# Shorter TensorE times in the clock estimate that orders a two-layer decoder's issue

## The chip, the core and the metric

The kernel runs on one core of a Trainium2 chip. The metric is the device time of one execution in microseconds (us), the median of several runs. One further execution was recorded by the hardware profiler; all rows below come from that one. The engines are TensorE (PE; its weight loads are PEld), VectorE (DVE), ScalarE (ACT), GpSimd (POOL) and SyncE (SP), which issues the DMAs.

## What is computed

Two residual layers over x of 2048 positions and 1024 channels, `x = x + rms_norm(mixer(rms_norm(x)))` each. Layer 0 projects to 2304 columns and has two head groups: sliding-window attention (8 query heads, 2 key/value heads, window 128, ALiBi, sinks) and a pooling mixer with windows 2, 4, 8 and 16; each is gated by a SiLU, and an output projection joins them. Layer 1 is a convolution module: a projection to 3072 columns, GLU, a causal depthwise convolution of 31 taps, a LayerNorm over channels, SiLU, a SiLU gate and an output projection:

```
proj = h @ w_in
a, b, gate = split(proj)
conv = depthwise_causal_conv(a * sigmoid(b), dw_w, 31 taps) + dw_b
y = silu(layer_norm(conv)) * silu(gate)
return y @ w_out
```

All data is float32.

## The kernel before, in words

Channels lie on partitions, 128 a tile (8 tiles), and positions in the free dimension, in two halves of 1024 with two blocks of 512 each. A projection of one output tile and one block (`project`, L385) runs over the 8 input tiles and issues three matmuls for each: weights and activations are split into a high and a low float32r part, and high by high, high by low and low by high are added into one PSUM bank. So a projection has 24 matmuls of 512 columns; the last block of the kernel is done in two parts of 256 columns (`last_block`, L1011). After each group of three matmuls `flow.pump()` lets other work in.

The order of the big work is written out: layer 0 for each half (36 projections with attention and pooling, then 16 of the output), layer 1's input for each half (32 projections of 8 channel tiles for GLU, then 16 gates), then layer 1's output for each half. Everything else is a task, a Python generator with a priority: weight loads and splits (`w_load`, `w_split`, priority 0), what reads a bank (0), attention (`scores`, `weighted`, 2), post-norm (`post_norm`, 1), the norm of the convolution (`norms`, L1158, 1 and 2), the convolution. Five of the eight channel tiles are convolved on DVE (`conv_dve`, L1027, priority 4: 31 taps over 128x1024, the first two as tensor_scalar, then 29 multiply-adds, and a sum), three on TensorE with Toeplitz matrices loaded by DMA (`conv_pe`, L1048, priority 2). `norms` of a half needs that half's convolution for all 8 tiles, sums them, takes the mean with matmuls and gives the input of the output projection, which waits for it tile by tile through `ready`.

The instructions are issued in the order in which this program calls them, each engine's in a queue of its own, with no other reordering. That order is decided by `Flow`, a running estimate of each engine's clock. Every operation's call adds its cost (`Engine.cost`, L156) to its engine's clock, not before its inputs' estimated ends (`note`, L78); it returns the estimated end, and a task yields that time. `once` (L123) goes through the tasks by priority and runs the first that is allowed:

```
ready = task[3]
if ready is not None and ready + MARGIN > self.t["P"]:
    continue
if task[0] > 0 and max(self.t["V"], self.t["A"]) > self.t["P"] + LAG:
    continue
```

Here `t["P"]`, `t["V"]` and `t["A"]` are the clocks of TensorE, DVE and ACT, MARGIN is 0.2 us and LAG 1.0 us. `wait` (L141), with which the main order waits for buffers and inputs, runs tasks until its condition holds and moves TensorE's clock on when none may run. The costs are in us. Beside TensorE's: a DVE operation on n elements a partition costs 0.063 + 1.04e-3 n, plus 0.067 for each per-partition scalar operand, half the slope for copies and tensor_scalar in SBUF; a DMA is taken as landed 0.65 + bytes/360e3 + 0.95 us after its issue if the queue is free (384 KB: 1.09 us in the middle).

All engine calls go through one helper, so every instruction of the profile has the line L189; tiles are told apart by name: `mm` a projection's bank, `wh` and `wl` split weights, `s` general tiles, `a`, `pt`, `pv` banks of attention, statistics and convolution, `in_toep` the Toeplitz matrices.

Of the kernel before, what the change touches and what calls it, by code (L numbers as in the profile page):

```python
# [53 lines left out]
class Flow:  # L54
# [17 lines left out]
    def keys(ap):  # L72
# [3 lines left out]
        return [(ap.name, c) for c in range(lo // 256, hi // 256 + 1)]  # L76

    def note(self, e, cost, ins, outs):  # L78
        s = self.t[e]
        for x in ins:  # L80
# [71 lines left out]
class Engine:  # L152
# [3 lines left out]
    def cost(self, op, out, ins, kw):  # L156
        n = 1
        for d in out.shape[1:]:
            n *= d
        psum = any(x.space == PSUM for x in ins + [out])  # L160
        ptr = 0.067 * sum(1 for x in ins if n > 1 and x.shape[-1] == 1)
        if self.key == "P":
            if op == "transpose":
                return 0.109
            f = ins[0].dtype
            if f == F32R:
                return max(0.111, 0.007 + 0.224 * n / 512)
            if n * out.shape[0] < 256:
                return 0.108
            part = 0.56 if out.shape[0] == 64 else 1.0  # L170
            return part * n * 1.74e-3
        if self.key == "V":
            if op == "reciprocal":
                return 0.06 + n * 6.25e-3
            fast = op in ("tensor_copy", "tensor_scalar") and not psum
            return 0.063 + ptr + n * (0.52e-3 if fast else 1.04e-3)
        if self.key == "A":
            return (0.052 if psum else 0.093) + 1.4 * ptr + n * 0.833e-3 + (0.09 if kw.get("accum_out") is not None else 0.0)
        if kw.get("op") == ALU.pow:
            return 1.0  # L180
        if op == "tensor_tensor":
            return 0.1 + n * 2.2e-3
        return 0.1 + n * 3.4e-3
# [1162 lines left out]
```

## Time and profile before

| | us |
|---|---|
| median of 3 runs (1518.21 to 1519.53) | 1518.54 |
| the profiled execution, its own time | 1523.78 |
| its span, first to last instruction | 1521.2 |
| TensorE busy in the span | 1477.2 |
| DVE busy | 1247.4 |
| ACT busy | 564.4 |
| GpSimd busy | 56.8 |

The span is what the trace shows; the profiled execution's own time has a little around it, and the unprofiled runs are somewhat shorter. Matmuls are pipelined, so the mean duration of one record is longer than the step from one to the next; the step is read from long pieces of the chain of waits. "x" is a count. A float32 matmul (not float32r) leaves two records. The release of a wait (`<-`) names what came last.

### The profile page before, as it was taken

What the parts mean: (1) busy time and instruction counts of PE and PEld (TensorE: products, weight loads), DVE (VectorE), ACT (ScalarE), POOL (GpSimd) and SP (SyncE); (2) the same over time, 40 slices, a digit from 0 to 9 for tenths busy, and PEclk for the clock granted to TensorE, in tenths of its full rate; (3) what the DMA queues carried; (4) which work ended last, traced back from release to release, by engine and by line L of the source; (5) the groups of instructions that cost most, each with busy time, mean ns of one, the idle gap of its engine ahead of it and who ended that gap; (6) DMA issues with size and microseconds to landing.
All of it is one profiled execution on the core that took longest, in us unless ns stands there. A gap on an engine that the chain in (4) does not pass through costs nothing.

```text
span 1521.2 us, 19133 instructions
## 1 busy us (share of the span) xinstructions
PE 1477.2 (97%) x7226; PEld 1192.8 (78%) x7226; DVE 1247.4 (82%) x1927; ACT 564.4 (37%) x1069; POOL 56.8 (4%) x65
## 2 busy tenths in 40 slices
PE   8999999999999999999999999999899999999997
PEld 6777788787777778787788878888788788788887
DVE  7887775776877755576799999969999799899975
ACT  6455422554444323454211113311112235375541
POOL 0000000000000000000100000000000002000000
PEclk9999999999999999999999999999999999999998
DMA  6122112464411111355421234431644654846764
GB/s 223 47 91 96 44 44 60 137 189 157 142 32 32 41 33 56 104 174 180 155 61 62 69 88 161 125 97 42 192 133 133 190 184 134 250 156 191 238 221 140
DMA packets 107468, 186.46 MB, mean 123 GB/s; under 512 B 32240, under 2 KB 56432, under 8 KB 107376
## 3 DMA queue, kind: packets, MB, share of 16 engines
q1 hardware_dynamic: 107376, 185.25, 38.7%
q8 instruction: 56, 0.92, 0.3%
q14 instruction: 36, 0.29, 0.1%
HBM read 146.42 MB, written 38.80 MB: 122 GB/s over the span
## 4 chain that ended last, share of the span: by engine, by line
PE 65%; DVE 23%; DMA 6%; issue 3%; ACT 2%; SPq 1%; POOL 0%; POOLq 0%; DVEq 0%; ACTq 0%
PE mm L189 56%; DVE s L189 18%; PE a L189 4%; PE pv L189 3%; DVE wl L189 2%; PE pt L189 2%; DVE t L189 2%; DMA s<-in_toep 2%; DMA xr<-in_xp 1%; ACT s L189 1%; SPq L189 1%; ACT t L189 1%; DMA gt<-s 1%; DMA xr<-x 1%; ACT wh L189 0%
## 5 line engine op out<-in xcount | busy, mean ns | idle before, releaser
L189 PE MATMUL mm<-s,wh 128*128 128x512 f32 (+1 forms) x3616 | 1138.6, 396 | 9.7 <-ACT s L189 6.2
L189 PEld LDWEIGHTS mm<-s,wh 128*128 128x128 f32 x3616 | 669.7, 189 | 159.3 <-ACT s L189 7.8
L189 PE MATMUL mm<-s,wl 128*128 128x512 f32 (+1 forms) x1808 | 710.9, 393 | 0.5 <-DVE wl L189 0.5
L189 PEld LDWEIGHTS mm<-s,wl 128*128 128x128 f32 x1808 | 341.6, 189 | 77.5 <-DVE wl L189 0.9
L189 DVE SCALAR_TENSOR_TENSOR s<-s,packed,s 128x1024 f32<-128x1024 f32 x290 | 354.3, 1282 | 0.0
L189 ACT ACTIVATE wh<-wr 128x1024 fp32r<-128x1024 f32 (+1 forms) x138 | 145.2, 1052 | 349.0 <-PE mm L189 319.7
L189 DVE TENSOR_TENSOR wl<-wr,wh 128x1024 fp32r<-128x1024 f32 (+1 forms) x138 | 167.5, 1214 | 82.3 <-ACT wh L189 82.1
L189 ACT ACTIVATE t<-mm 128x512 f32<-128x512 f32 (+1 forms) x122 | 68.6, 562 | 107.2 <-PE mm L189 94.0
L189 PE MATMUL a<-s,s 128*128 128x128 f32 (+2 forms) x592 | 94.9, 297 | 10.9 <-DMA s<-in_toep 8.1
L189 DVE TENSOR_TENSOR t<-t,t 128x512 f32<-128x512 f32 (+1 forms) x131 | 85.8, 662 | 20.0 <-ACT t L189 18.2
L189 PEld LDWEIGHTS a<-s,s 128*128 128x128 f32 x592 | 82.6, 194 | 24.8 <-DMA s<-in_toep 11.7
L189 DVE TENSOR_TENSOR s<-s,s 128x512 f32<-128x512 f32 (+3 forms) x100 | 85.3, 873 | 6.9 <-DMA s<-sg 2.1
L189 ACT ACTIVATE s<-t 128x512 fp32r<-128x512 f32 (+1 forms) x52 | 48.8, 938 | 110.1 <-DVE t L189 109.6
L189 ACT ACTIVATE s<-mm 128x512 f32<-128x512 f32 (+1 forms) x116 | 67.9, 586 | 52.1 <-PE mm L189 49.0
L189 ACT ACTIVATE t<-s 128x512 f32<-128x512 f32 x80 | 49.3, 629 | 58.7 <-DVE s L189 50.3
L189 DVE TENSOR_TENSOR s<-t,s 128x512 fp32r<-128x512 f32 (+1 forms) x56 | 52.1, 930 | 23.1 <-ACT s L189 22.1
L189 DVE TENSOR_TENSOR t<-pt,packed 128x512 f32<-128x512 f32 x64 | 44.2, 690 | 31.4 <-PE pt L189 31.2
L189 POOL TENSOR_TENSOR rs<-ms,mhalf 128x4 f32<-128x4 f32 (+1 forms) x21 | 29.4, 1398 | 800.4 <-DVE ms L189 800.4
L189 ACT ACTIVATE s<-s,st 128x128 f32<-128x128 f32 x128 | 49.7, 390 | 22.2 <-DVE st L189 22.0
L189 DVE SCALAR_TENSOR_TENSOR s<-t,mm 128x512 f32<-128x512 f32 x48 | 39.9, 831 | 14.9 <-PE mm L189 13.7
L189 ACT ACTIVATE s<-xh 128x512 fp32r<-128x512 f32 x48 | 30.2, 632 | 51.2 <-DVE xh L189 50.6
L189 DVE TENSOR_TENSOR s<-s,xr 128x512 f32<-128x512 f32 x56 | 37.5, 687 | 7.5 <-DMA xr<-x 4.7
(100 smaller groups left out, 917.9 us busy)
## 6 DMA issues: line engine op xcount, KB each, us to landing
wr<-in_wo SPq DMA_DIRECT2D x64, 512.0 KB, 3.7
wr<-in_wc SPq DMA_DIRECT2D x48, 512.0 KB, 3.7
wr<-in_wa SPq DMA_DIRECT2D x27, 512.0 KB, 3.8
s<-in_toep SPq DMA_DIRECT2D x24, 384.0 KB, 4.5
xr<-in_xp SPq DMA_DIRECT2D x32, 256.0 KB, 4.0
x<-s SPq DMA_DIRECT2D x32, 256.0 KB, 3.1
xh<-x SPq DMA_DIRECT2D x32, 256.0 KB, 3.1
sg<-s SPq DMA_DIRECT2D x16, 512.0 KB, 5.0
```

The source lines that it names most:

```text
L189: fn(*args, **kw)
```

## The change

In the cost of a TensorE operation the three constants of the matmuls are replaced; the cost of a transpose (0.109) and of the smallest matmuls (0.108) stay, and so do all costs of the other engines, MARGIN, LAG and all instructions.

```diff
             f = ins[0].dtype
             if f == F32R:
-                return max(0.111, 0.007 + 0.224 * n / 512)
+                return max(0.107, 0.2148 * n / 512)
             if n * out.shape[0] < 256:
                 return 0.108
             part = 0.56 if out.shape[0] == 64 else 1.0
-            return part * n * 1.74e-3
+            return part * n * 1.67e-3
```

## Rows read from the trace of the kernel before

**Rows 1.** The page's first part: busy us, share of the span, instructions.

```profile
PE 1477.2 (97%) x7226; PEld 1192.8 (78%) x7226; DVE 1247.4 (82%) x1927; ACT 564.4 (37%) x1069; POOL 56.8 (4%) x65
```

**Rows 2.** Stretches: window and length; PE, PEld, DVE, ACT, POOL busy; PEclk, DMA share, GB/s.

```profile
0.00:170.80 170.80, 161.12 (x882) 123.32 (x883) 142.93 (x403) 91.77 (x239) 5.63 (x16) 1.00 0.31 102
366.90:528.80 161.90, 159.29 (x912) 123.95 (x911) 125.25 (x361) 68.59 (x194) 2.21 (x3) 1.00 0.20 63
744.00:994.70 250.70, 246.68 (x1067) 199.06 (x1066) 250.46 (x243) 52.16 (x74) 18.92 (x15) 1.00 0.32 99
994.70:1213.60 218.90, 210.85 (x1034) 174.58 (x1032) 188.05 (x164) 38.58 (x74) 1.44 (x7) 0.99 0.43 128
1213.60:1309.90 96.30, 96.30 (x434) 77.92 (x434) 93.65 (x116) 40.75 (x68) 7.74 (x2) 1.00 0.52 168
```

**Rows 3.** The chain of waits, three undisturbed pieces: start us, us, engine and tile.

```profile
546.16 78.11 PE mm L189 x336
...
1215.22 1.34 PE a L189 x12
...
1490.22 18.43 PE mm L189 x156
```

**Rows 4.** The waits of TensorE: who, for whom, us in total, times, longest.

```profile
PE a L189 <- DMA s<-in_toep: 8.1, 8, 2.7
...
PE a L189 <- DVE s L189: 5.8, 9, 2.8
PE pv L189 <- DVE s L189: 4.4, 2, 2.5
PE mm L189 <- DVE s L189: 3.6, 4, 1.9
PE pt L189 <- DVE t L189: 3.4, 4, 1.4
```

**Rows 5.** The timeline of TensorE at two waits: start, us, instruction [idle before, releaser].

```profile
907.63 1.10 PE L189 MATMUL pv<-s,onesr 128*128 128x512 f32 x2 [2.48 <-DVE s L189]
...
1459.06 0.39 PE L189 MATMUL mm<-s,wh 128*128 128x256 f32 x1 [1.87 <-DVE s L189]
```

**Rows 6.** Groups of DVE, 768.2 to 879.3 us: count, busy us, mean ns, idle before.

```profile
L189 DVE SCALAR_TENSOR_TENSOR s<-s,packed,s 128x1024 f32<-128x1024 f32 x73 | 88.9, 1284 | 0.0
L189 DVE TENSOR_TENSOR wl<-wr,wh 128x1024 fp32r<-128x1024 f32 x10 | 12.2, 1222 | 0.0
L189 DVE SCALAR_TENSOR_TENSOR s<-t,mm 128x512 f32<-128x512 f32 x10 | 8.6, 865 | 0.0
L189 DVE TENSOR_TENSOR s<-s,s 128x1024 f32<-128x1024 f32 x2 | 4.0, 2024 | 0.1
L189 DVE TENSOR_SCALAR s<-s,packed 128x1024 f32<-128x1024 f32 x4 | 2.9, 775 | 0.0
```

**Rows 7.** The timeline of DVE before 907 us: start us, us, instruction, count.

```profile
900.41 1.04 DVE L189 SCALAR_TENSOR_TENSOR s<-t,mm 128x512 f32<-128x512 f32 x1
901.28 4.86 DVE L189 SCALAR_TENSOR_TENSOR s<-s,packed,s 128x1024 f32<-128x1024 f32 x4
906.05 1.00 DVE L189 SCALAR_TENSOR_TENSOR s<-t,mm 128x512 f32<-128x512 f32 x1
```

**Rows 8.** Three more stretches, columns as in rows 2.

```profile
1003.00:1014.00 11.00, 11.00 (x49) 8.94 (x48) 2.26 (x2) 1.55 (x2) 0.00 (x0) 1.00 0.46 168
1014.00:1205.00 191.00, 183.80 (x900) 152.15 (x898) 179.00 (x156) 32.74 (x64) 1.39 (x6) 0.99 0.43 126
1213.60:1454.80 241.20, 238.38 (x1055) 192.66 (x1055) 225.36 (x312) 127.73 (x201) 12.09 (x6) 0.99 0.61 195
```

**Rows 9.** Groups of TensorE's 512-column matmuls, 1213.6 to 1454.8 us.

```profile
L189 PE MATMUL mm<-s,wh 128*128 128x512 f32 x640 | 202.2, 397 | 0.0
L189 PE MATMUL mm<-s,wl 128*128 128x512 f32 x320 | 126.1, 394 | 0.0
```

**Rows 10.** The page's DMA issues, Toeplitz loads: count, KB, median us to landing.

```profile
s<-in_toep SPq DMA_DIRECT2D x24, 384.0 KB, 4.5
```

## The prediction, made before the change was run

> **What bounds the kernel now.** I began with the engines' shares of the span. TensorE is busy for 97% of it and VectorE (DVE) for 82% [rows 1]: the reader should take from this that no other order of issue can win much, since the matmuls stay the same. Next came the stretches between the phases [rows 2]. In the attention of layer 0 (0 to 171 us, 367 to 529 us) TensorE is idle for 9.7 and 2.6 us, the first with the start of the kernel in it, and DVE has time to spare; from 744 to 995 us, in layer 1's first projection and gates, both are nearly full, DVE 250.5 of 250.7 us; in the second projection TensorE loses 8 us; in the gate stretch (1214 to 1310 us) TensorE is never idle and DVE is at 97%. So from 744 us on there are two nearly full engines, and how their work is interleaved matters; before that TensorE is the bound alone.
>
> Third, the chain of waits for long undisturbed pieces, to see what a matmul costs [rows 3]: 336 matmuls of 512 columns take 78.11 us, 0.2325 us each; 156 of 256 columns take 18.43 us, 0.118 each; twelve float32 records take 1.34 us, and as one float32 matmul leaves two records, that is 0.223 each. The old estimate books 0.231, 0.119 and 0.2227 (128 columns): it is right within 1%. The new one books 0.2148, 0.1074 and 0.2138, too short by 7.6% (0.2325/0.2148 = 1.082; old 1.006; the quotient 1.076) for nearly all matmuls. The change makes an accurate estimate wrong.
>
> Last, who makes TensorE wait [rows 4], with two single waits [rows 5]: 8.1 us in 8 waits for the Toeplitz loads; 5.8, 3.6 and 3.4 us, 17 waits, for DVE results in short operations and operands; 4.4 us in 2 waits of the row broadcast, of which 2.48 at 907 us. The last block's matmuls wait 1.87 us at 1459 us.
>
> **The change part by part.** No instruction is added or removed; the scheduler decides with shorter matmul times where each engine's instruction stands in its queue. Two rules of it use TensorE's clock. A task's next step is issued once that clock is 0.2 us past the time its input should be ready; so the step lands behind more matmuls than now, 7.6% more for the same wait (for a chain that it books at 5 us: 23.3 matmuls in place of 21.6). And a task of lower priority is held while DVE's or ACT's clock is 1 us ahead of TensorE's; so DVE gets less optional work per matmul. The first helps TensorE, the second holds DVE back.
>
> First term, short operations that wait for DVE. The three rows of 5.8, 3.6 and 3.4 make 12.8 us in 17 waits, 0.75 us on average [rows 4]. With chains of some 5 us (an estimate: four or five DVE operations of about 0.9 to 1.2 us, as in [rows 7]) the cover grows by 7.6% of 5, 0.38 us, or 6.4 us in 17 waits; a wait shorter than 0.38 can't give that much, so I take 5. Bounds 0 (a step is only considered after every third matmul, 0.69 us apart, so some land where they were) and 12.8.
>
> Second term, the wait at 907 us. Between 768.2 and 879.3 us DVE issues 73 convolution steps, 10 splits of weights and 10 GLU products [rows 6]. The plan books 1.195, 1.128 and 0.595 each (from the cost formula), and 5.1 us for the six further ones (two sums at 1.128, four first taps at some 0.7): 87.2 + 11.3 + 6.0 + 5.1 = 109.6 us. The 480 matmuls there (five channel tiles of 96) book 110.9 us now. So the plan fills DVE to 99%. The true steps: four convolutions start 4.77 us before the next operation, 1.19 each, as booked; but a GLU product holds the queue for 0.87 us [rows 7], not 0.595. DVE is thus a little over-filled, slides behind, and the broadcast at 907 us stands behind what is queued [rows 5]. After the change the same matmuls book 103.1 us, DVE is given 6.5 us less (5.9%), and the slide is gone: 2.5 us won, bounds 0 and 2.5.
>
> Third term, the Toeplitz loads. The plan takes a load as landed 0.65 + 1.09 + 0.95 = 2.7 us after its issue, the row says 4.5 us [rows 10]. 7.6% of 2.9 us (with the margin) is 0.22 us a wait, 1.8 us for eight; bounds 0 and 8.1.
>
> Fourth term, what DVE is not given. The 5.9% are 14.8 us of the full 250.7 us from 744 to 994.7 us [rows 2], and 10.6 us of the 179.0 that it works from 1014 to 1205 us [rows 8]. What covers this: DVE idles 8.7 us between 1003 and 1014 us and 12.0 us in the second stretch [rows 8], it seems for want of the next tile; a backlog fills just these. 14.8 - 8.7 leaves 6.1, with 10.6 makes 16.7, less 12.0 is 4.7 us of convolution that arrives late in the last stage. That stage, 1213.6 to 1454.8 us, has no cover: 960 matmuls [rows 9] book 221.8 us now, with 11.9 us of the stage's short ones (broadcasts, statistics, Toeplitz products, counted in the code) 233.7 in all, and 206.2 + 11.4 = 217.6 after. DVE's work there is 225.4 us busy [rows 8], in the plan's booking 1% to 3% less, 219 to 223. Now the plan has 11 to 15 us to spare for DVE; after, it lacks 1 to 5 us. The last convolution tile, at the lowest priority, then ends later in the order; the second half's norm starts behind it; and the last block's matmuls, which wait for that norm, are late next. The true DVE idles 15.8 of the 241.2 us, so part is absorbed. I take 3 us of loss; bounds 9.7 (4.7 carried and 5 lacking, nothing absorbed) and a gain of 6, as 241.2 us hold only 235 us of matmuls at the true rate (960 at 0.2325 and 11.9).
>
> No DMA is added; loads that stand in the order behind a step move with it on SyncE's queue. GpSimd's queue has a few small steps and sees no bound. Waits for the start and the tail after the last matmul stay.
>
> Sum: -5 - 2.5 - 1.8 + 3 = -6.3 us. The profiled execution took 1523.78 us, 2.6 us around its span of 1521.2, and 5.2 us over the median of the runs, 1518.54; on it the sum gives 1517.5, on the median 1512.2. I predict **1512**.
>
> One rule speaks on the estimate itself. The row's 0.2325 us per 512 columns [rows 3] stands. The Trainium skill, "TensorE: Matmul & The Clock Gate", section "Back-to-back issue gap", gives N/2.4 + 2.5 ns when warm, 215.7 ns for 512 columns, which is the new estimate; by that the new booking would be the true one, no step would land behind more matmul time than it needs, and the first three terms would be nothing. The trace does not agree, although the granted clock in the two stretches with the longest runs of matmuls is 1.00, the 2.4 GHz level [rows 2].
>
> **The rivals.** (a) DVE becomes the bound of the last stage: slower. Place: the last convolution tile and the second half's norm between 1214 and 1455 us; price: the full 9.7 us, against half of the first three terms, 4.7, so +5.0 us, 1523.5. It decides from the point where the norm's last splits, against the matmuls, come over 4.7 us later than now: TensorE waits for them already [rows 5], so nothing covers it there. For it: DVE is at 97% from 1214 to 1310 us [rows 2], and the plan loses all its slack. Against it: the real DVE is not held by the plan's clock, only its order is changed.
>
> (b) No change. Steps are considered only every three matmuls, the gains stay at half (4.7 us) and the last stage takes 3 to 5 back: 1517 to 1519. For it: the waits at stake are 24 us of 1521, most below a microsecond. The Trainium skill's rule, as a mechanism that matmuls stream at 0.2148 us when no profile is taken, would end here as well (0.02 of its chance): the 960 of the last stage alone would then run 17 us shorter than at 0.2325, and the median of the whole is only 5 us below the profiled time.
>
> (c) The order hardly changes, so that it does nothing at all: hardly possible, since every comparison with TensorE's clock moves by up to 7%; it is part of (b).
>
> **How the numbers follow.** The forecast, gains outweigh, 1505 to 1515.5: 0.50. Rival (a): 0.26, reaching from 1521.6 to 1528 (all of 9.7 lost, nothing gained). Rival (b) with (c): 0.24. About 0.2%, 3 us, is what a measurement can tell from no change; the three cases are cut there. The range for 8 in 10 goes from 1504 (first three terms at 12, last one a gain of 2) to 1526; the forecast's own range is 1505 to 1515.5.
>
> **What would show it.** Right: matmul pieces still at 0.2325 us; the wait at 907 us gone and DVE with idle pieces between 744 and 995 us; Toeplitz waits of 5 to 7 us in place of 8.1; the three DVE rows at about 8 us in place of 12.8; the wait for DVE before the last block (1459 us now) longer than its 1.9 us. Wrong: if the short operations' waits stay as long, the first term fails; if the last convolution ends no later against the gate projections, or DVE's idle time from 1214 us falls, the fourth does; a wait of over 8 us at the last block or at the second block of the first half's output is rival (a).

## The result, and the profile after

The changed kernel takes **1501.49 us** (median of 4 runs, 1500.89 to 1503.71); the kernel before, run beside it, 1519.03. The ratio is 0.9886, with a 95% interval of 0.9869 to 0.9903: faster by 17.5 us, where 6.5 were forecast. The sign was right; the size was nearly three times the forecast and lies 2.5 us below the range. The profiled execution took 1503.71 us around a span of 1500.8. The span went from 1521.2 to 1500.8, 20.4 us less; but the profiled execution of the kernel before lies 4.8 us above its median and that of the changed one 2.2 above, so about 2.5 of the 20.4 belong to the executions and not to the change.

The first part of the page after the change, to be held against [rows 1] (busy us, share, instructions):

```profile
span 1500.8 us, 19112 instructions
...
PE 1469.3 (98%) x7226; PEld 1193.0 (79%) x7226; DVE 1250.2 (83%) x1927; ACT 565.2 (38%) x1069; POOL 49.1 (3%) x65
```

The work is the same, to the instruction; TensorE's busy sum fell by 7.9 us all the same. To see where time was won, I took the start of the first matmul of each stage from the timelines of both kernels and of every experiment:

| us | before | after | difference |
|---|---|---|---|
| layer 0, until layer 1 begins | 719.7 | 709.2 | -10.5 |
| layer 1, first half: input and gates | 274.9 | 267.5 | -7.4 |
| layer 1, second half: input ("second projection") | 218.9 | 206.7 | -12.2 |
| second half's gates and the first outputs ("last stage") | 241.2 | 256.5 | +15.3 |
| last block and tail ("rest") | 66.4 | 60.9 | -5.5 |
| span | 1521.2 | 1500.8 | -20.4 |

So 30.2 us are won before the second half's gates (the "front", 1213.6 before and 1183.4 after), and 9.8 given back behind it. Each number is of one execution. Two experiments below have the same order of issue up to the gates as one of these kernels, and their fronts are 1210.2 (old times, `e12_new_at_end`) and 1181.2 (new times, `e5_old_at_end`): a difference of 2 to 3 us between fronts says nothing. The stretches that answer to [rows 2] and [rows 8] (window and length; PE, PEld, DVE, ACT, POOL busy; PEclk, DMA share, GB/s):

```profile
0.00:163.45 163.45, 156.86 (x842) 123.11 (x843) 134.07 (x376) 86.27 (x218) 4.86 (x15) 1.00 0.31 102
364.05:519.58 155.53, 155.13 (x894) 122.25 (x893) 125.29 (x360) 65.12 (x182) 2.46 (x4) 1.00 0.21 65
737.00:976.70 239.70, 239.70 (x1051) 196.30 (x1050) 232.02 (x224) 49.82 (x71) 13.72 (x13) 1.00 0.32 101
976.70:1183.40 206.70, 205.67 (x1010) 170.70 (x1008) 196.46 (x172) 37.95 (x71) 1.75 (x7) 1.00 0.43 128
1183.40:1439.90 256.50, 247.67 (x1079) 199.00 (x1079) 234.35 (x320) 131.10 (x208) 8.15 (x6) 0.97 0.59 189
1439.90:1500.80 60.90, 50.03 (x415) 49.50 (x413) 39.77 (x70) 20.47 (x42) 2.40 (x3) 0.92 0.56 189
```

Read the third line against its partner in [rows 2]: TensorE, idle for 4.0 us before (250.70 - 246.68), is idle for none, and DVE, which had no idle time, now has 7.7 us. In the second projection TensorE's idle time fell from 8.1 to 1.0 us. The fifth line is the loss: TensorE idle 8.8 us where [rows 8] leave 2.8, DVE 9.0 us busier, and the granted clock 0.97 in place of 0.99.

The waits of TensorE up to the gates (for whom; total, times, longest), first before, 0 to 1213.6 us, then after, 0 to 1183.4 us; of before, four lines that [rows 4] don't have:

```profile
PE mm L189 <- ACT s L189: 6.2, 3, 5.5
...
PE a L189 <- DVE s L189: 3.0, 8, 0.9
PE pv L189 <- DVE s L189: 2.5, 1, 2.5
PE pv L189 <- DVE t L189: 1.9, 5, 0.5
```

```profile
PE mm L189 <- ACT s L189: 6.9, 4, 5.4
PE pv L189 <- DVE t L189: 2.2, 3, 1.2
PE mm L189 <- DVE s L189: 1.3, 2, 0.6
PE a L189 <- DMA s<-in_toep: 0.9, 2, 0.7
PE a L189 <- DVE s L189: 0.2, 1, 0.2
```

Gone are nearly all of the 8.1 us for the Toeplitz loads and all of the 3.4 for `pt` [rows 4], the 2.5 us of the broadcast [rows 5] and 2.8 of the short operations' 3.0. All waits up to the gates sum to 27.4 us before and 11.5 after. That is 15.9 of the 30.2 us: half of the gain was never shown as idle time of TensorE.

### The profile page after: what moved, and what is told of

It reads as the page before. It is cut to its first block, busy times and chain, and to the rows that moved or that the text cites. A ratio compares the mean times of both kernels' runs of the same rounds, so it can differ in the third digit from the quotient of the medians.

```text
span 1500.8 us, 19112 instructions
## 1 busy us (share of the span) xinstructions
PE 1469.3 (98%) x7226; PEld 1193.0 (79%) x7226; DVE 1250.2 (83%) x1927; ACT 565.2 (38%) x1069; POOL 49.1 (3%) x65
## 4 chain that ended last, share of the span: by engine, by line
PE 92%; DVE 3%; DMA 2%; ACT 1%; issue 1%; SPq 0%; POOL 0%; POOLq 0%; DVEq 0%; ACTq 0%
PE mm L189 81%; PE a L189 5%; PE pv L189 3%; PE pt L189 2%; DVE s L189 2%; DMA s<-in_toep 1%; DVE t L189 1%; DVE wl L189 0%; DMA s<-in_xn 0%; DMA gt<-s 0%; ACT s L189 0%; DMA s<-sg 0%; SPq L189 0%; ACT wh L189 0%; ACT t L189 0%
## 5 line engine op out<-in xcount | busy, mean ns | idle before, releaser
L189 PE MATMUL a<-s,s 128*128 128x128 f32 (+2 forms) x592 | 90.5, 290 | 1.1 <-DMA s<-in_toep 0.9
L189 POOL TENSOR_TENSOR rs<-ms,mhalf 128x4 f32<-128x4 f32 (+1 forms) x21 | 24.9, 1186 | 791.8 <-DVE ms L189 787.7
L189 PEld LDWEIGHTS pv<-t,s 128*64 128x64 f32 x480 | 25.1, 136 | 23.2 <-issue 7.2
```

Of the source, the lines that this page charges most:

```text
L189: fn(*args, **kw)
```

## The experiments

All times are medians, and each ratio stands to the kernel before on the same chip. "Front" is the start of the second half's gates, as in the table. Where an expectation calls a theory by a letter, the sentences around it say in words what was at issue.

### What won the front: cover, hold or margin?

The shorter times do two things: a step lands behind more matmuls (cover), and optional DVE and ACT work is held back (hold). Two kernels part them. A second pair of clocks for DVE and ACT, `pace`, serves in the hold alone; with costs scaled by 0.93, the changed kernel keeps its cover but holds no more than before (`e2_cover`); with 1.076 in the kernel before, the hold comes without the cover (`e3_hold`).

```diff
-LAG = 1.0
+LAG = 0.93
+PACE = 0.93
...
+        if e in self.pace:
+            self.pace[e] = max(self.pace[e], s) + cost * PACE
...
-            if task[0] > 0 and max(self.t["V"], self.t["A"]) > self.t["P"] + LAG:
+            if task[0] > 0 and max(self.pace.values()) > self.t["P"] + LAG:
```

> The new matmul times, but the hold on lower priorities compares a second pair of DVE and ACT clocks whose costs are scaled by 0.93 (and LAG by the same), so that these tasks are held as they were before the change; only the readiness test sees the shorter matmuls. Theory A (the gain comes from steps that land behind more matmuls, the loss at the end from holding DVE back): faster than the changed kernel, 1488 to 1497 us, Toeplitz waits about 1 us as after the change, and the wait of about 4 us in layer 1's output at 1385 us much shorter. Theory B (the gain comes from holding the lower priorities longer, which delays their short matmuls): back near the kernel before, 1512 to 1520 us, with Toeplitz waits of 6 to 8 us.

> The old matmul times, but the hold on lower priorities sees DVE and ACT costs times 1.076 (LAG times the same), as the change makes them stand to TensorE's; the readiness test is as before. Theory A: no gain in the first 1210 us, Toeplitz waits of 6 to 9 us, and the convolution late at the end: 1519 to 1530 us. Theory B: 1500 to 1508 us with Toeplitz waits of 1 to 3 us.

Cover alone: 1512.74 us, ratio 0.9965 (0.9953 to 0.9977), front at 1191.3, 22.3 us early, and no wait for a Toeplitz load is left up to there. Hold alone: 1556.75 us, 1.0249 (1.0234 to 1.0264), front at 1209.9, within what one order varies (1213.6 and 1210.2), with 9.0 us of Toeplitz waits. So the cover wins three quarters of the front, and up to there theory A (cover) is right. Its other half is not: with cover alone the total falls into the range of theory B, since the last stage is as long without the extra hold as with it (257.9 and 256.5 us).

```profile
1191.30:1449.20 257.90, 245.53 (x1079) 197.68 (x1078) 230.87 (x316) 129.31 (x206) 9.25 (x6) 0.96 0.57 186
```

So the last stage's loss needs no extra hold. What the cover lacks without the hold is seen in its timeline at the start of the second projection (start, us, instruction, idle before and releaser), two waits that the changed kernel hasn't:

```profile
990.02 0.49 PE L189 MATMUL mm<-s,wh 128*128 128x512 f32 x1 [2.61 <-ACT s L189]
...
993.01 0.80 PE L189 MATMUL mm<-s,wh 128*128 128x512 f32 x1 [2.50 <-DVE s L189]
```

The second half's activations are not ready there: in DVE's queue six convolution steps (7.25 us from 981.39 us) stand before what makes them. Hold alone makes the last stage 285.0 us; its line of that stage and its longest wait:

```profile
1209.90:1494.90 285.00, 246.12 (x1055) 195.86 (x1054) 233.55 (x319) 129.97 (x204) 9.22 (x6) 0.92 0.53 172
```

```profile
1317.15 0.79 PE L189 MATMUL mm<-s,wl 128*128 128x512 f32 x1 [10.82 <-DVE wl L189]
```

A constant cover, the kernel before with a larger margin:

```diff
-MARGIN = 0.2
+MARGIN = 0.6
```

> The kernel before with MARGIN 0.6 in place of 0.2 us: every step of a task comes 0.4 us later against TensorE, while all costs and so the share of DVE stay as they were. Theory A: most of the gain up to 1214 us comes with this alone, Toeplitz waits 1 to 3 us, and there is no late wait in layer 1's output: 1490 to 1505 us. Theory B: 1514 to 1522 us.

1507.08 us, 0.9927 (0.9912 to 0.9941): two thirds of the whole gain, without touching a cost. But by another way: the front gains 8.7 us only, with 5.1 us of Toeplitz waits left, and the last stage loses nothing (239.6 us, clock 1.00). That is neither theory's forecast: A asked for most of the front and Toeplitz waits of 1 to 3 us. The fixed cover does not replace the one that grows with the length of the chain.

Which constant, and is it proportional? One kernel takes only the float32r line of the change, another the two constants of before times 0.965, half the step:

> One part alone: only the float32r constant (the projections) is the new one; the float32 one (attention, statistics, Toeplitz products) stays. If the gain comes from projections booked too short, against which the short steps are placed: 1499 to 1506 us, Toeplitz waits below 2 us. If the float32 times matter as much, since they book the steps that wait themselves: 1508 to 1516 us.

> Half the dose: both old constants times 0.965 (0.223 us for 512 columns). Theory A (cover, in proportion): about half of the 30 us won ahead of the second half's gates, that stage starting at 1195 to 1202 us in place of 1214 (before) and 1183 (changed), and a total of 1505 to 1512 us. If the order of issue falls well or badly by chance rather than in proportion, that stage starts outside of 1188 to 1208 us.

The float32r line alone gives the whole front (1183.9), with 1.5 us of Toeplitz waits, and 1509.10 us, 0.9942 (0.9927 to 0.9957). That total is in the second range, for another reason than that range was given for: the rest is 6.3 us longer than with the whole change (67.2), and the rest takes 60.5 to 73.3 us over the kernels of this study, without a pattern that I see. Half the step gives 1510.06, 0.9954 (0.9936 to 0.9972), and four fifths of the front (1189.0, 24.6 of 30.2). The gain isn't proportional: steps are considered after every third matmul, so they move in groups of three. Counted in the issue order, between a Toeplitz load and its first use lay 17.25 matmuls of 512 columns on average before and 24.25 in the changed kernel; but this mean is raised by a few long ones (medians 15 and 19.5), and with the float32r line alone it is 18.75. The short ones tell more: six of the 24 loads were issued nine matmuls before their first use; with the float32r line alone the same six stand 12 or 15 matmuls before it, in the changed kernel 12 to 66. One group of three is 0.70 us, where the third term reckoned 0.22.

### What costs at the end

Old times from the second half's gates on, new before (`e5_old_at_end`), and the mirror of it (`e12_new_at_end`):

```diff
+    fast = True
...
-                return max(0.107, 0.2148 * n / 512)
+                return max(0.107, 0.2148 * n / 512) if self.flow.fast else max(0.111, 0.007 + 0.224 * n / 512)
...
+        flow.fast = half + 1 < NH
         gates1(half, now)
```

> The new matmul times up to the gates of the second half of layer 1, the old ones from there. If the loss in layer 1's output comes from the new times in the last stage itself: 1488 to 1496 us, the wait at 1385 us gone. If it comes from the convolution that was put off earlier (the backlog at the start of that stage), or from DVE's own work, it stays at 1499 to 1504 us with that wait still 3 us or more.

> The mirror of the earlier run: the old matmul times up to the gates of the second half of layer 1, the new ones from there. If the last stage is long because TensorE comes to it 30 us earlier than before and DVE's work is then not as far: that stage (gates to the last block) takes 236 to 246 us as before (241) and the total is 1510 to 1522 us. If it is long because the new times give DVE too little and in a worse order in that stage: 252 to 262 us as after the change (256), total 1528 to 1540 us.

The longest wait of the first in its last stage, and the stage of the second:

```profile
1346.82 1.40 PE L189 MATMUL pv<-s,onesr 128*128 128x512 f32 x2 [7.77 <-DVE s L189]
```

```profile
1210.20:1462.80 252.60, 244.49 (x1056) 195.63 (x1055) 228.38 (x316) 128.53 (x203) 8.47 (x6) 0.96 0.59 189
```

New times at the end alone make the kernel slower than before: 1527.35 us, 1.0061 (1.0042 to 1.0080), last stage 252.6 in place of 241.2. Old times at the end don't mend the changed kernel: 1508.63, 0.9939 (0.9922 to 0.9956), last stage 263.9, with the 7.8 us at a broadcast that the line shows. So both cost the stage something by themselves: the new booking in it 11.4 us, TensorE's early arrival 22.7 (263.9 - 241.2); together they give 15.3, so they don't add. The first run missed both of its expectations, and each difference carries the chance of order that the last part of this section shows, some 6 us either way.

Is it DVE's work? The adds that sum the squares in three full blocks of layer 1's output are left out, some 12.6 us of DVE, in the changed kernel and in the one before:

```diff
-            V.tensor_tensor(out=box[0], in0=box[0], in1=q, op=ALU.add)
+            if lat is None:
+                V.tensor_tensor(out=box[0], in0=box[0], in1=q, op=ALU.add)
...
-        yield from sum_squares(box, bank)
+        yield from sum_squares(box, bank, lay or None)
```

> The changed kernel without the DVE additions that collect the squares of layer 1's output in its three full blocks (7 of 0.60 us each, so 12.6 us less DVE work there; the sums of squares are left incomplete). If DVE's work is the bound of the last stage after the change: waits of TensorE for DVE there fall from 8.8 us to below 4, and the total by 6 to 14 us, to 1487 to 1496 us. If other links (the order, weight splits, loads) set it: 1497 to 1505 us.

> The same additions left out of the kernel before (12.6 us less DVE work in layer 1's output), as the control. If DVE's work is a bound of the last stage only after the change: 1515 to 1520 us, that stage 238 to 243 us. If it bounds that stage before the change as well: 1508 to 1514 us.

The last stage of both, after the change and before it:

```profile
1181.60:1433.10 251.50, 244.98 (x1079) 197.56 (x1078) 224.69 (x302) 130.29 (x207) 10.71 (x6) 0.97 0.61 195
```

```profile
1213.60:1455.90 242.30, 239.07 (x1055) 192.34 (x1055) 216.54 (x297) 128.25 (x204) 13.00 (x6) 0.99 0.61 197
```

Each has about 9 us less DVE work in the stage. The changed kernel's stage gains 5.0 us (1495.93, 0.9851, 0.9836 to 0.9867, against 1501.49), and TensorE's waits for DVE in it fall from 8.3 to 3.3 us; the stage of the kernel before gains nothing (241.2 to 242.3; 1517.53, 0.9980, 0.9969 to 0.9991). Both are as forecast for a load of DVE that counts in the last stage only after the change. But 5.0 us are within the chance of order, so this is likely and not shown; and as only half of the work taken out comes back, DVE's load isn't the only bound.

Twenty of the 31 taps of the last convolved tile left out of the changed kernel (`e7_less_dve_new`), and that tile's priority raised from 4 to 1 (`e6_last_conv_first`), test whether its lateness sets the end:

```diff
-        for k in range(2, CK):
+        for k in range(2, CK - 20 if half and i == 7 else CK):
```

```diff
-            flow.spawn(conv_dve(half, i, slot, gl, over), 4)
+            flow.spawn(conv_dve(half, i, slot, gl, over), 1 if half and i == 7 else 4)
```

> The changed kernel without 20 of the 31 taps of that one tile's second-half convolution (its values are left incomplete): 24 us less DVE work in the last stage, nothing less on TensorE. If DVE's work bounds the last stage since TensorE comes 30 us earlier: the waits of layer 1's output shrink to below 3 us in all and the total falls by 9 to 15 us, to 1486 to 1493 us. If the order of TensorE's short steps makes that wait: 1497 to 1502 us.

> The changed kernel, but the last tile's convolution on DVE in the second half has priority 1 in place of 4. If the wait of layer 1's output at 1385 us comes from this tile's being put off behind all else: 1486 to 1496 us, and the wait gone. If it comes from DVE's work as a whole, which is full there in any order: 1499 to 1506 us, with the wait in this or another place.

By its total the first is in the second range (the order), by its waits in the first (0.6 us in the last stage); the other run missed both. The first one's last stage and rest:

```profile
1181.80:1421.80 240.00, 239.41 (x1079) 194.73 (x1079) 206.84 (x293) 126.32 (x202) 7.44 (x6) 1.00 0.61 198
...
1421.80:1495.10 73.30, 55.77 (x415) 53.23 (x413) 44.52 (x77) 23.23 (x48) 2.73 (x3) 0.84 0.49 170
```

With 24 us of DVE work less (20 taps of 1.2) the last stage is back at 240.0 us, at clock 1.00 and with 0.6 us idle, but the rest grows from 60.9 to 73.3 at a lower clock, and 1497.48 us (0.9865, 0.9849 to 0.9882) is only 4 better than the changed kernel: the waits moved to the last block (8.9 us there, 2.3 in the changed kernel). Its counterpart in the kernel before wasn't tried, so this run settles nothing by itself.

With that tile first the kernel loses 19.5 us on the changed one (1521.03, 1.0015, 1.0005 to 1.0024). Its timeline shows where (start, us, instruction, idle before and releaser): at the norm and the projections behind the gates.

```profile
1284.70 1.63 PE L189 MATMUL pt<-ones,t 128*128 128x1 f32 x8 [2.94 <-DVE t L189]
1290.84 1.30 PE L189 MATMUL pv<-s,onesr 128*128 128x512 f32 x2 [3.44 <-DVE s L189]
...
1317.25 0.79 PE L189 MATMUL mm<-s,wh 128*128 128x512 f32 x1 [8.78 <-DVE s L189]
```

DVE's timeline shows what stands before the longest of these waits (8.78 us):

```profile
1307.22 10.58 DVE L189 TENSOR_TENSOR s<-s,s 128x512 fp32r<-128x512 f32 x10
```

Seven of the ten are 128x1024, 8.6 us: the adds over the eight tiles of the second half, whose last tile is convolved at about 1240 us here and 1293 us in the changed kernel. Done early, the tile lets these adds in where the first half's norm is still due. The tile's low priority is not what costs.

DVE waits for ACT's high parts (`wl` for `wh`) 15.0 us in the last stage after the change (the expectation says 13.9), 4.0 before:

```profile
DVE wl L189 <- ACT wh L189: 15.0, 18, 3.1
```

```profile
DVE wl L189 <- ACT wh L189: 4.0, 7, 1.3
```

A microsecond more before DVE's part of a split is allowed:

```diff
-                yield A.activation(wh[:, ks], raw[:, ks], AF.Copy)
+                yield 1.0 + A.activation(wh[:, ks], raw[:, ks], AF.Copy)
```

> The changed kernel, with the DVE half of each weight split issued 1.0 us later by the estimate (so behind more of DVE's other work). Theory H: in the last stage DVE stands still 13.9 us at the head of its queue on split weights whose ACT half still waits for TensorE to free a buffer, because TensorE's matmuls are booked too short there; then these waits fall below 6 us and the total to 1490 to 1497 us. Theory D (DVE's work itself is the bound and those waits are only slack that shows up there): 1499 to 1504 us.

> The same edit in the kernel before, where DVE waits 4.0 us for these splits in the last stage: both theories 1514 to 1521 us, as the control for the edit's own effect on the order.

The wait fell to 4.3 us as meant, and the time did not: 1505.79, 0.9917 (0.9894 to 0.9940), last stage 255.8; in the kernel before 1521.91, 1.0013 (1.0001 to 1.0025). DVE's waits for the splits are slack. That theory (H) falls.

### How much is chance of order, and a better setting

The new float32r slope up and down by 0.7%, and the new costs with a larger margin:

```diff
-                return max(0.107, 0.2148 * n / 512)
+                return max(0.107, 0.2163 * n / 512)
```

> The changed kernel with 0.2163 us for 512 columns in place of 0.2148 (0.7% more). If the result goes by the size of the constant: 1499 to 1504 us. If the order in the last stage is an accident of small shifts: the gates of the second half still start at 1180 to 1190 us, but the total lies anywhere from 1492 to 1515 us, most of the difference in the last stage.

> The same with 0.2133 us (0.7% less). By the size of the constant: 1499 to 1504 us; by accident in the last stage: gates at 1178 to 1188 us and a total anywhere from 1492 to 1515 us.

> The changed kernel with MARGIN 0.6 in place of 0.2. Theory A (cover): with the new times the cover is already enough, so up to the second half's gates there is little left (that stage starts at 1178 to 1186 us, 1183 in the changed kernel). In the last stage the steps of DVE's chain come later: 1500 to 1510 us. If cover was still missing anywhere: 1490 to 1498 us.

> The same with MARGIN 0.4: between the two, the gates of the second half at 1178 to 1186 us, total 1496 to 1508 us; a total outside of that would show that the last stage goes by the accidents of the order more than by either knob.

| kernel | median us | ratio (95%) | front | last stage |
|---|---|---|---|---|
| slope 0.2163 | 1502.41 | 0.9895 (0.9879 to 0.9910) | 1184.6 | 251.1 |
| slope 0.2133 | 1511.33 | 0.9952 (0.9935 to 0.9969) | 1187.6 | 262.3 |
| margin 0.6 | 1497.30 | 0.9852 (0.9833 to 0.9870) | 1178.2 | 253.3 |
| margin 0.4 | 1507.81 | 0.9925 (0.9907 to 0.9943) | 1181.7 | 263.7 |

The front is firm: with the new booking, in any of these, it begins between 1178 and 1188. The last stage is not: 0.7% of a constant either way makes it 251.1 or 262.3 us, as the second theory of these two runs has it, so some 6 us either way are chance of order. Their lines tell where it goes, first slope 0.2163, then 0.2133:

```profile
1184.60:1435.70 251.10, 246.68 (x1079) 199.40 (x1078) 228.28 (x313) 127.94 (x204) 8.42 (x6) 0.97 0.60 193
```

```profile
1187.60:1449.90 262.30, 249.58 (x1068) 199.18 (x1067) 236.29 (x322) 129.46 (x204) 8.02 (x6) 0.94 0.58 188
```

TensorE is idle 4.4 us in the one and 12.7 in the other, and the granted clock is 0.97 and 0.94; 0.03 and 0.06 of the stage are 7.5 and 15.7 us (the two overlap, as TensorE also waits while the clock is low). The stage's length goes with the clock over the whole study: 240 us at 1.00 (margin 0.6 or the later splits in the kernel before, 20 taps less in the changed one), 241 and 242 at 0.99, 251 to 274 at 0.97 to 0.94, 285 at 0.92. Margin 0.6 on top of the change is the fastest full kernel of the study, 4.2 us below the changed one; their intervals just meet, and with margin 0.4 ten us worse I don't call it a rule.

## Why the prediction was right in sign and wrong in size

In short: the way of the gain, cover for short steps and loads, was right. The terms that priced it were too small, 9.3 us in all for a front that won about 30: they took the rows of waits as all that could be won, and a cover of a few tenths of a microsecond a wait, where a step moves by whole groups of 0.70 us. The granted clock was put at nothing, and it counts on both sides. The fourth term was right in sign, but the hold, by which it was reckoned, isn't needed for the loss.

**First and second terms** (-7.5 together). The mechanism is right: the cover run alone wins most of the front, the wait at 907 us is gone, and DVE has idle pieces before the gates. The size is not. Layer 0 and layer 1's first half won 17.9 us. The step that failed is the ceiling: I took the wait rows as all there was to win, 12.8 and 2.5 us, and gave the cover a share of them; but half of the front's gain shows in no wait. (Of the 12.8, only 7.5 stood before the gates; 1.5 of them are left. The three rows sum to 9.8 after the change, forecast 8, since 8.3 us of new waits stand in the last stage.) Part of what the rows hide can be read. A wait costs more than its row: before, the matmul ahead of the broadcast starts at 904.75 us (first line), a step of 0.23 would put the broadcast at 904.98, and it starts at 907.63 [rows 5]: 2.65 lost, 2.48 shown.

```profile
904.75 0.40 PE L189 MATMUL mm<-s,wl 128*128 128x512 f32 x1
```

At 0.17 each, the 22 waits fewer up to the gates (34 before, 12 after) give an estimated 3.7 us. The Trainium skill, "Perfetto Trace Analysis", section "Per-instruction lifecycle: what the profiler-reported window actually captures", says that for TensorE the profiler estimates the end of an instruction from its size and does not observe it; no run here can tell such an end from an observed one.

Then the clock. In the front of the kernel before TensorE runs twice at a granted clock of 0.50, the lower of its two levels (1.2 GHz), behind a wait of 1.1 us at 707.5 us and one of 2.7 us for a Toeplitz load at 1080 us:

```profile
708.70:712.10 3.40, 3.40 (x9) 2.62 (x8) 0.93 (x4) 0.00 (x0) 1.01 (x1) 0.50 0.55 152
1080.80:1084.20 3.40, 3.40 (x18) 3.40 (x17) 0.83 (x1) 0.00 (x0) 0.00 (x0) 0.50 0.55 208
```

Half of 6.8 us is 3.4 us lost, all counted as busy. In the front of the changed kernel there is no such stretch. Not every wait has one behind it: after the 2.48 us at 907 us the clock stays at 1.00 (905 to 925 us). The Toeplitz products of the second half show the loss, before (994.7 to 1309.9 us) and after (976.7 to 1282.4), count, busy, mean ns, idle before:

```profile
L189 PE MATMUL a<-s,s 128*128 128x128 f32 x288 | 38.0, 286 | 8.1 <-DMA s<-in_toep 8.1
```

```profile
L189 PE MATMUL a<-s,s 128*128 128x128 f32 x288 | 35.9, 276 | 1.0 <-DMA s<-in_toep 0.9
```

Most of the 2.1 us are that one stretch: the 24 records behind the wait at 1080 us take 4.57 us, where 24 of 0.111 take 2.7.

A third part I had excluded in words: "matmul pieces still at 0.2325 us". In the long pieces of the chain of waits they are shorter after the change. Layer 1's first half before, then layer 0 and layer 1's first half after (start, us, engine, tile, count):

```profile
908.72 38.18 PE mm L189 x165
...
947.61 69.42 PE mm L189 x300
```

```profile
542.89 73.66 PE mm L189 x318
...
748.03 145.27 PE mm L189 x633
```

In layer 0 that is 0.2325 [rows 3] before and 0.2316 after, in layer 1's first half 0.2314 and 0.2295. If it holds for all matmuls there, 0.0009 for some 2450 and 0.0019 for 1152 make 2.2 us each, an estimate. The granted clock is 1.00 in all four. Other kernels with the new times have 0.2302 to 0.2317 there in pieces of over 100 us; what sets it stays open. Waits (15.9), what the rows hide of them (3.7), clock (3.4), step (4.4) and moved records (2.7, see the third term) make 30.1 of the 30.2 us; that it comes so close is luck, as two executions of one order differ by 2 to 3. Even so the matmul is 7 to 8% longer than it is booked, so the new estimate wins by being wrong. The Trainium skill, "TensorE: Matmul & The Clock Gate", section "Back-to-back issue gap", gives N/2.4 + 2.5 ns warm for a matmul by itself, some 216 ns for 512 columns, and about 131 ns for a stream of weight loads and matmuls. By the first the booking would be true; the trace agrees with neither, after the change as before.

**Third term** (-1.8): the term that was missed most. Its waits fell from 8.1 to 0.9 us, not to 5 to 7, and the second projection won 9.5 us net of some 2.7 that only moved (24 records of Toeplitz products, 0.111 each, now stand behind the gates' start). Besides the 7.2 us of waits it won the 1.7 us of the low clock at 1080 us. The step that failed is "7.6% of 2.9 us, 0.22 us a wait". A step is considered after every third matmul, and a load that misses a point waits for the next: the six loads that stood nine matmuls before their use moved by at least one group, 0.70 us. A row with the landing time was at hand: the loads take 4.5 us [rows 10] and the plan books 2.7, so what they lacked was about 1.8.

**Fourth term** (+3, bounds -6 to +9.7): right in place and in sign. The last stage lost 15.3 us, 12.6 of them net of the moved records, above the bound. The rest gave 5.5 back, but not by what the term reckons: the rest of the kernel before takes 60.7 us in the run without the additions, so the 66.4 may be that one execution. What I had right: work is carried in (DVE 9.0 us busier there, 4.7 forecast), and the last convolved tile ends later against the gates (at 1293 us, 110 us into the stage, where it was 92). The step that failed is the title of the term, "what DVE is not given": with cover alone DVE is held no more than before, and the stage is 257.9 us all the same (hold alone makes it 285.0). It loses as well when TensorE comes to it 22 to 30 us earlier (cover alone, and old times at the end), or when its own booking is short (new times at the end). That DVE's load is then a bound is likely and not shown; it idles 22.2 of the 256.5 us, more than the 15.8 before. What I left out besides is a price that TensorE pays for a wait beyond it. Two stretches of the changed kernel, columns as above:

```profile
1381.00:1385.30 4.30, 0.61 (x3) 0.20 (x3) 4.14 (x7) 2.18 (x4) 0.00 (x0) 1.00 0.84 265
1385.50:1402.50 17.00, 14.14 (x38) 10.23 (x38) 14.05 (x27) 6.93 (x11) 2.83 (x2) 0.50 0.35 125
```

The first is nearly all one wait of 3.7 us for DVE, ahead of a statistic:

```profile
1385.28 1.68 PE L189 MATMUL pt<-ones,t 128*128 128x1 f32 x8 [3.69 <-DVE t L189]
```

Behind it TensorE runs for 17 us at a granted clock of 0.50; it is busy for 14.1 of them and so loses 7.1. The stage of the kernel before loses 1.7 us in this way, behind its wait of 2.8 us at 1328.9:

```profile
1330.00:1333.40 3.40, 3.40 (x8) 1.99 (x7) 3.40 (x6) 2.28 (x5) 0.00 (x0) 0.50 1.03 420
```

So the stage's 15.3 us are 2.7 moved, 6.0 of waits and 5.4 of clock, 14.1 in all.

The forecast that the wait before the last block would grow from 1.9 us was wrong: it is gone, and the rest ran 5.5 us shorter, at clock 0.92, where the kernel before has

```profile
1454.80:1521.20 66.40, 53.16 (x415) 52.23 (x413) 40.28 (x71) 21.34 (x44) 2.73 (x3) 0.87 0.51 169
```

The loss had come out earlier, in the middle of the stage. Rival (a) named the right place: hold without cover makes the kernel 2.5% slower, and the new booking in the last stage alone 0.6%. Its mechanism, a full DVE, is not what these show: with hold alone DVE is busy for 233.55 of the stage's 285.0 us, and TensorE waits for single results that come late in the order. In the whole change the rival is outweighed, since the first three terms, which it halved, were some 27 us.

Open: what sets the last stage's length in detail. Priorities and splits don't, less DVE work may in part, and 0.7% of a constant up or down puts it 11 us apart, in waits and in the clock behind them.

## What to carry to other kernels

Where a program orders in-order queues by an estimate, the truest estimate need not be the best. Here it paid to book the bottleneck engine short, so that short steps land behind more of its work: an operand that came late cost TensorE its wait, a part that no wait row shows, and sometimes its clock. So look for the granted clock behind each wait before you take the rows of waits as all there is to win. Look separately at the stage where another engine is nearly as full; there the same booking cost 11 us. Judge such a constant by several settings around it, as one setting carries some 6 us of chance here.

## What was not expected of the hardware

Waits of 0.9 and 3.7 us within 5 us, in a full stream of matmuls, were followed by 17 us at a granted clock of 0.50, about 7 us lost, twice the longer wait. In the kernel before, waits of 1.1, 2.7 and 2.8 us were each followed by a short stretch at 0.50 (1.7 us lost in each), and one of 2.5 us by none. And the step between float32r matmuls of 512 columns was 0.2295 to 0.2317 us in the long pieces of layer 1's first half in kernels that differ only in order, 0.2325 in layer 0 of the kernel before, all at a granted clock of 1.00.
